# An encoder trunk in which the Strassen token blocks of the FFN become quarters of each half

## The chip, the cores and the metric

The kernel runs on one core of a Trainium2 chip. The metric is the device time of one launch in microseconds (us); the kernel before was timed in three runs. TensorE (PE) multiplies matrices and accumulates in eight PSUM banks; VectorE (DVE), ScalarE (ACT) and GpSimd (POOL) do the elementwise work, POOL without access to PSUM; SyncE (SP) issues the DMAs between HBM and the on-chip memory (SBUF). Each engine takes its instructions in the order of its own queue.

## The reference, cut

1024 tokens, model width 1024, two layers (differential attention, then neighbourhood attention), FFN width 2816, fp32.

```python
h = x
for i in range(DEPTH):
    hn = rmsnorm(h, norm_mix[i])
    ...
    h = h + mix                       # mix = attention output @ w_o
    h = h + swiglu(rmsnorm(h, norm_ffn[i]), ffn_w_gate[i], ffn_w_up[i], ffn_w_down[i])
    gate = jax.nn.sigmoid(rmsnorm(h, norm_ple[i]) @ ple_w_gate[i])
    h = h + gate * (p[i] @ ple_w_proj[i])
return rmsnorm(h, norm_final)
```

`swiglu(h)` is `(silu(h @ w_gate) * (h @ w_up)) @ w_down`.

## The kernel before

Activations lie with features on the 128 partitions and tokens along the free dimension: `h` is eight tiles of [128, 1024], handled in two halves of 512 tokens. An fp32 operand is split into a rounded part and a remainder (`split`: a cast on ACT or POOL, then a subtraction on DVE), and every product of 128x128 weights with 512 tokens is three passes on PE (`PASSES`).

*Output projection.* Attention makes eight head pairs `u`; each pair's output goes to DRAM (`ot`), the last stays in SBUF (`self.last`). `out_proj_first` multiplies the first six pairs (`EARLY`) by their part of `w_o` for both halves, while the last heads are still at work, adds the residual and stores to `hp`. `out_proj` does the last two pairs: first all eight output tiles of half 0, then those of half 1, and behind each half its norm (`norm_blocks`). `norm` sums the squares of the eight tiles on DVE, takes the inverse root and broadcasts it by a PE product (`sums`, `bc`), and makes the normed tiles one by one.

*Gate and up* (`gate_up`) are products by Strassen's scheme in seven products instead of eight (`ORDER`, `seven`): weights are cut into 2x2 blocks (`blocks`), and so are the normed activations, the rows being feature tiles k and k + 4, the columns the two token halves. So five of the seven operands `bt[b]` need half 1. For each of eleven pairs of hidden tiles there are two groups (gate, up) of 84 products of 512 columns; `hand_over` forms the seven operands of down and stores them to DRAM (`ad`), seven DMAs of 512 KB a pair.

*Down* (`down`) works in five chunks of hidden pairs: for each it loads the operands `b` (22 buffers, 14 loads for a chunk of two pairs) and then for four pairs of output tiles the raw weights, which `blocks` turns into seven.

*What sets the order.* Tiles come from pools. Pools take addresses as a stack from the left of SBUF, or with `side="right"` from the right, and give them back when they close; a tile takes slot 0 of its tag first and then the last slot downwards. All DMAs are issued on SP's one queue. A planner orders each engine's queue ahead of time, from costs of its own; among what it holds ready, earlier in the program goes first. In the built program the first instruction of a pool stands, without an exception, behind the last instruction of every earlier pool whose addresses it takes; `reuse_waits="tile"` makes an instruction wait at run time only for the tiles that it overlaps itself. In `gate_up`, `gw` (raw weights and split weights) lies at the bottom of the left stack, over `ob` (`self.last`), `ho` (h of the output projection) and `no` (its norm); `gt` (gates and the other small tiles) lies above, over `oin` (operands and weights of the late products) and `so` (their staging tiles). In `down`, `h` and `pw` lie over `gw`; `db` (operands) over `gt` and three of the `bt` tiles; `dw` (raw and split weights) over `bt` tiles alone.

Lines of the change: `norm` 114, `norm_blocks` 147, `out_proj_first` 554 (its products are L572, its adds L574), `out_proj` 578 (L597), `gate_up` 604 (L631), `down` 690 (L719, loads L706 and L710), `build`. Helpers record one line for many tiles: L101, L103 and L104 are the splits, L190 the blocks of weights.

## Time and profile before

| | us |
|---|---|
| median of three runs | 3028.1 (3024.58 to 3028.22) |
| the profiled execution | 3023.98, its span 3022.2 |
| PE busy | 2739.8 (91%) |
| PE weight loads busy | 2255.1 (75%) |
| DVE busy | 2130.2 (70%) |
| ACT busy | 1217.8 (40%) |
| POOL busy | 1325.6 (44%) |
| DMA | 379.59 MB, 126 GB/s over the span |

A share is an average over stages. PE runs through most of the span without a gap; where it stands still is seen in the timeline, that is the list of an engine's instructions in order of time, neighbours of one kind merged. A line there has the start, the time from the first to the last of the merged ones, engine, line, operation, what is written and read, and in brackets the idle time before and whom the engine waited for. In the window table the figure behind an engine is its busy time in that stretch and in parentheses the instructions.

### The profile page before, as it was taken

How to read it: one execution, taken by the hardware profiler on the slowest of the kernel's cores; microseconds unless marked ns; L12 is line 12 of the kernel's file. 1: busy time of each engine (PE TensorE's matmuls, PEld its weight loads, DVE VectorE, ACT ScalarE, POOL GpSimd, SP SyncE). 2: the span in 40 equal slices, each digit the busy share in tenths (PEclk: the TensorE clock that was granted, in tenths of full speed). 3: DMA queues.
4: the chain of work that ended last, by engine and by line, in shares of the span. 5: the costliest groups of instructions: out<-in, count | busy, mean ns of one | idle time of the engine just before them, and what ended most of it. 6: DMA issues, size and time to landing. Idle time of an engine off the chain costs nothing. (4 is left out here: it accounts for less than half of the span.)

```text
span 3022.2 us, 38402 instructions
## 1 busy us (share of the span) xinstructions
PE 2739.8 (91%) x13272; PEld 2255.1 (75%) x13272; DVE 2130.2 (70%) x3947; ACT 1217.8 (40%) x2534; POOL 1325.6 (44%) x1240
## 2 busy tenths in 40 slices
PE   6999999997599999599997999999399999789998
PEld 5787888885477878478786888888287788567876
DVE  6798878776767666498584666765866667568766
ACT  4454546443444443233332544542344344323241
POOL 1344443431555555477221443432255555457621
PEclk8999999998799999799998999999699999989999
DMA  3001010324244443866132112144333444486312
GB/s 114 28 29 42 29 42 27 147 100 160 63 153 141 145 154 133 313 258 251 35 119 82 54 69 75 47 170 163 117 116 143 153 153 153 159 330 252 138 63 105
DMA packets 106321, 379.59 MB, mean 126 GB/s; under 512 B 12176, under 2 KB 14352, under 8 KB 102032
## 3 DMA queue, kind: packets, MB, share of 16 engines
q1 hardware_dynamic: 106128, 377.15, 34.5%
q8 instruction: 105, 1.72, 0.2%
q14 instruction: 88, 0.72, 0.1%
HBM read 256.52 MB, written 120.59 MB: 125 GB/s over the span
## 5 line engine op out<-in xcount | busy, mean ns | idle before, releaser
L631 PE MATMUL mm<-bt,w 128*128 128x512 f32 x3696 | 870.4, 397 | 62.6 <-ACT w L101 59.6
L631 PEld LDWEIGHTS mm<-bt,w 128*128 128x128 f32 x3696 | 695.2, 189 | 240.2 <-ACT w L101 62.7
L719 PE MATMUL mm<-b,w 128*128 128x512 f32 x1848 | 432.8, 395 | 72.0 <-DMA b<-ad 63.2
L719 PEld LDWEIGHTS mm<-b,w 128*128 128x128 f32 x1848 | 348.1, 190 | 156.8 <-issue 65.2
L104 DVE TENSOR_TENSOR w<-raw,w 128x512 fp32r<-128x512 f32 (+2 forms) x420 | 356.2, 865 | 50.8 <-ACT w L101 50.4
L219 PE MATMUL d<-hnT,w 128*128 128x512 f32 x1536 | 386.3, 399 | 0.0
L219 PEld LDWEIGHTS d<-hnT,w 128*128 128x128 f32 x1536 | 287.0, 189 | 64.3
L101 ACT CAST w<-raw 128x512 fp32r<-128x512 f32 (+2 forms) x420 | 210.6, 527 | 213.0 <-POOL raw L190 109.2
L103 POOL TENSOR_SCALAR w<-st 128x1024 fp32r<-128x1024 f32 (+2 forms) x120 | 134.3, 1121 | 335.5 <-PE mm L219 100.9
L294 PE MATMUL d<-w,hnT 128*128 128x256 f32 x1536 | 227.2, 294 | 16.0 <-POOL w L103 7.7
L294 PEld LDWEIGHTS d<-w,hnT 128*128 128x128 f32 x1536 | 210.5, 198 | 27.7 <-POOL w L103 9.3
L725 POOL TENSOR_TENSOR h<-h,u 128x512 f32<-128x512 f32 x120 | 169.4, 1426 | 119.0 <-DVE u L725 118.4
L104 DVE TENSOR_TENSOR w<-s,w 128x512 fp32r<-128x512 f32 (+2 forms) x168 | 123.4, 749 | 126.4 <-ACT w L101 126.4
L190 POOL TENSOR_TENSOR s<-raw 128x512 f32<-128x512 f32 (+2 forms) x84 | 95.3, 1134 | 267.2 <-DMA raw<-gu 221.0
L366 ACT ACTIVATE e<-e,mx 128x1024 f32<-128x1024 f32 x128 | 147.3, 1151 | 124.7 <-DVE mx L364 113.4
L104 DVE TENSOR_TENSOR w<-st,w 128x1024 fp32r<-128x1024 f32 (+2 forms) x120 | 136.7, 1141 | 82.4 <-POOL w L103 81.4
L219 PE MATMUL mm<-hnT,w 128*128 128x512 f32 x768 | 188.5, 406 | 4.8 <-ACT hnT L101 3.2
L219 PEld LDWEIGHTS mm<-hnT,w 128*128 128x128 f32 x768 | 147.1, 193 | 45.4 <-issue 7.4
L101 ACT CAST at<-tr 128x512 fp32r<-128x512 f32 (+2 forms) x288 | 132.0, 481 | 106.2 <-PE tr L515 67.5
L281 PE MATMUL s<-kh,qs 128*128 128x512 f32 (+2 forms) x384 | 153.4, 409 | 23.2 <-DVE mx L358 12.6
L104 DVE TENSOR_TENSOR at<-tr,at 128x512 fp32r<-128x512 f32 (+2 forms) x288 | 155.7, 550 | 22.5 <-ACT at L101 16.7
L381 POOL TENSOR_SCALAR e<-e,rc 128x1024 f32<-128x1024 f32 x64 | 74.2, 1160 | 217.3 <-DVE rc L379 212.1
(144 smaller groups left out, 4608.1 us busy)
## 6 DMA issues: line engine op xcount, KB each, us to landing
ad<-put SPq DMA_DIRECT2D x154, 512.0 KB, 2.8
b<-ad SPq DMA_DIRECT2D x154, 512.0 KB, 8.4
raw<-gu SPq DMA_DIRECT2D x88, 512.0 KB, 4.8
raw<-wd SPq DMA_DIRECT2D x32, 512.0 KB, 7.3
st<-wpg SPq DMA_DIRECT2D x32, 512.0 KB, 3.6
ot<-ot SPq DMA_DIRECT2D x14, 1024.0 KB, 3.9
o<-ot SPq DMA_DIRECT2D x14, 1024.0 KB, 7.9
st<-da_qk SPq DMA_DIRECT2D x16, 512.0 KB, 3.4
```

Source lines behind the costliest of these rows:

```text
L101: hi_engine.copy(out=w[0], in_=src)
L103: hi_engine.tensor_scalar(out=w[0], in0=src, scalar1=1.0, scalar2=0.0, op0=ALU.mult, op1=ALU.add)
L104: self.nc.vector.tensor_tensor(out=w[1], in0=src, in1=w[0].bitcast(F32), op=ALU.subtract)
L190: nc.gpsimd.tensor_tensor(out=o, in0=x, in1=y, op=op)
L219: self.nc.tensor.matmul(ps, w[:, i, kt * P:(kt + 1) * P], self.hnT[half][:, j, kt, :], start=kt == 0 and n == 0, stop=kt == KT - 1 and n == 2)
L281: self.nc.tensor.matmul(s, qs[:, m, qc], (kh, kl)[part][:, m, kc], start=part == 0, stop=part == 1)
L294: self.nc.tensor.matmul(ps, self.hnT[t // 4][:, i, k, c], ws[k // 4][:, j, (k % 4) * 256:(k % 4 + 1) * 256], start=k == 0 and n == 0, stop ...
L366: nc.scalar.activation(out=e[m], in_=e[m], func=AF.Exp, bias=mx[:, m:m + 1], scale=SLOPES[h], accum_out=sm[:, m:m + 1])
L381: nc.gpsimd.tensor_scalar(out=e[0], in0=e[0], scalar1=rc[:, 0:1], scalar2=0.0, op0=ALU.mult, op1=ALU.add)
L631: nc.tensor.matmul(acc, w[b][:, i, k * P:(k + 1) * P], bt[b][:, j, k], start=first and k == 0 and n == 0, stop=k == 3 and n == 2, skip_gro ...
L719: nc.tensor.matmul(acc, w[b][:, i, q], mv[b, q][:, j], start=first and q == 0 and m == 0, stop=q == n - 1 and m == 2, skip_group_check=True)
L725: eng.tensor_tensor(out=o, in0=x, in1=y, op=ALU.add)
```

## The change

- **Token blocks.** The columns of the 2x2 blocks are no longer the two halves but the first and second quarter (256 tokens) within each half. So each half gives its own part of all seven `bt[b]`, now [128, 2, 4, 2, 256]; a product still takes 512 columns, a quarter from each half. `norm_blocks` is the same for both halves: it works on two tiles at a time, subtracts on DVE, and five of a norm's seven sums of squares go to POOL (`adder`).
- **First pair in parts.** For pair 0 of gate and up the groups run on half 0 first (`part` 0: 256 columns, gate, then up), then on half 1.
- **Output projection.** `out_proj_first` does half 0 alone. `out_proj` then does half 0's last two pairs and half 0's norm, and after that half 1 with all eight pairs, with weights read row-wise (`wn`, a second copy of `w_o`) in two passes over four output tiles each, three weight buffers and two staging buffers; then half 1's norm.
- **Down.** `db` is opened on the right, in the place of `bt`, and chunk 0's loads are issued ahead of `h`, `pT` and `wpp`, which `between` loads. `bt` is allocated in the order in which its tiles are last used.
- **Buffers** of `gate_up`: `raw` 3 to 2, split weights 10 to 14, `p5` and `u3` 2 to 1, `put` 3 to 2. With these sizes `gw` lies over all of `ob`, `ho`, `no` and the first tiles of `oin`; `gt` over the rest of `oin` and `so`. In `down` `h`, `pw` and the staging tile lie over `gw`, `dw` over `gt`, `dt` and `db` over `bt`. `so` (staging of the late weights) lies over attention's values.

```diff
-                nc.vector.tensor_tensor(out=acc[:, :w], in0=acc[:, :w], in1=sq[:, :w], op=ALU.add)
+                eng = adder if adder is not None and k < 6 else nc.vector
+                eng.tensor_tensor(out=acc[:, :w], in0=acc[:, :w], in1=sq[:, :w], op=ALU.add)
...
+        held = {}
+
+        def alloc(k):
+            if k % 2 == 0:
+                held[k // 4] = pool.tile([P, 2, HALF], F32, tag=f"n{k // 4}", name="n", bufs=2)
+            return held[k // 4][:, k % 2]
...
+            ks = slice(k % 4 - 1, k % 4 + 1)
+            lo, up = held[0], held[1]
+            b11, b12, b21, b22 = lo[:, :, :QUART], lo[:, :, QUART:], up[:, :, :QUART], up[:, :, QUART:]
+
+            def put(b, x):
+                self.split((bt[b][:, 0, ks, half], bt[b][:, 1, ks, half]), x, nc.scalar)
+
+            def sub(o, x, y):
+                nc.vector.tensor_tensor(out=o, in0=x, in1=y, op=ALU.subtract)
+
+            put(0, b11)
+            t2 = pool.tile([P, 2, QUART], F32, tag="t2", name="t2", bufs=1)
+            t3 = pool.tile([P, 2, QUART], F32, tag="t3", name="t3", bufs=1)
+            sub(t3, b22, b12)
+            sub(b12, b12, b11)
+            sub(t2, b22, b12)
+            put(5, t2)
+            put(4, b12)
+            put(1, b21)
+            put(6, t3)
+            sub(b21, b21, t2)
+            put(3, b21)
+            put(2, b22)
+
+        self.norm(h, c, i, pool, sink, order=(0, 1, 4, 5, 2, 3, 6, 7), alloc=alloc, adder=nc.gpsimd)
```

```diff
+            o = p.tile([P, 2, HALF], F32R, tag=f"o{u}", name="o")
+            nc.sync.dma_start(out=o.bitcast(F32), in_=self.ot[layer][u, :, :, :HALF])
...
+            r = p.tile([P, HALF], F32, tag="r", name="r", bufs=3)
+            nc.sync.dma_start(out=r, in_=self.residual(layer, dt)[:, :HALF])
+            acc = psd.tile([P, HALF], F32, tag="d", name="d")
...
+        last = self.last.rearrange("p l b q -> p l (b q)")
+        late = range(EARLY, PAIRS)
+        os = {}
+        for half, u in [(0, u) for u in late[:-1]] + [(1, u) for u in range(PAIRS - 1)]:
+            o = op.tile([P, 2, HALF], F32R, tag=f"o{half}{u}", name="o")
+            nc.sync.dma_start(out=o.bitcast(F32), in_=self.ot[layer][u, :, :, half * HALF:(half + 1) * HALF])
+            os[half, u] = o
+        for half in range(2):
+            os[half, PAIRS - 1] = last[:, :, half * HALF:(half + 1) * HALF]
+        h = {}
...
+                h[dt, half] = hpool.tile([P, HALF], F32, tag="h", name="h", bufs=12)
+                nc.sync.dma_start(out=h[dt, half], in_=self.hp[dt] if half == 0 else self.residual(layer, dt)[:, c])
...
+            if half == 0:
+                for dt in range(KT):
+                    w = self.weights(wo[dt, :, EARLY * P:], op, "w", cols=len(late) * P, bufs=3)
+                    acc = ps.tile([P, HALF], F32, tag="mm", name="mm")
+                    for u in late:
+                        k = u - EARLY
+                        product(acc, w[:, :, k * P:(k + 1) * P], u, k == 0, u == PAIRS - 1)
+                    done(dt, acc)
+            else:
+                for q in range(2):
+                    accs = [ps.tile([P, HALF], F32, tag="mm", name="mm") for _ in range(4)]
+                    for u in range(PAIRS):
+                        w = self.weights(wn[u * P:(u + 1) * P, q * HALF:(q + 1) * HALF], op, "w", cols=HALF, bufs=3)
+                        for d in range(4):
+                            product(accs[d], w[:, :, d * P:(d + 1) * P], u, u == 0, u == PAIRS - 1)
+                    for d in range(4):
+                        done(4 * q + d, accs[d])
+            self.norm_blocks(lambda k, c, half=half: h[k, half], half, 3 * layer + 1, np, bt)
```

```diff
-                    r = wp.tile([P, 2, HALF], F32, tag="raw", name="raw", bufs=3)
+                    r = wp.tile([P, 2, HALF], F32, tag="raw", name="raw", bufs=2)
...
-            def group(pr, which):
-                w = prepare(pr, which)
+                    gates[pr] = tp.tile([P, 2, 2, 2, QUART], F32, tag="gt", name="gt", bufs=2)
+                return self.blocks(raw[0][:, 0], raw[0][:, 1], raw[1][:, 0], raw[1][:, 1], wp, "w", [HALF], 14)
+
+            def block(gt, f, t, part):
+                return gt[:, f, :, t] if part is None else gt[:, f, part, t]
...
+                t = {k: tp.tile([P, 2, QUART], F32, tag=k, name=k, bufs=n)
+                     for k, n in (("p1", 2), ("p5", 1), ("u2", 2), ("u3", 1))}
+                cut = (lambda x: x) if part is None else (lambda x: x[:, part])
+                t = {k: cut(x) for k, x in t.items()}
...
-                            nc.tensor.matmul(acc, w[b][:, i, k * P:(k + 1) * P], bt[b][:, j, k],
+                            nc.tensor.matmul(cut(acc), w[b][:, i, k * P:(k + 1) * P], cut(bt[b][:, j, k]),
...
-                    o = tp.tile([P, 2, HALF], F32R, tag="put", name="put", bufs=3)
+                    o = tp.tile([P, 2, 2, QUART], F32R, tag="put", name="put", bufs=2)
...
+                if pr == 0:
+                    ws = [prepare(pr, which) for which in range(2)]
+                    for part in range(2):
+                        for which in range(2):
+                            group(pr, which, ws[which], part)
+                else:
+                    for which in range(2):
+                        group(pr, which, prepare(pr, which))
```

```diff
+                if chunk is CHUNKS[0]:
+                    between()
...
-                bt = [bp.tile([P, 2, 4, HALF], F32R, tag=f"b{b}", name=f"bt{b}") for b in range(7)]
+                bt = {b: bp.tile([P, 2, 4, 2, QUART], F32R, tag=f"b{b}", name=f"bt{b}") for b in ORDER}
...
+                    self.out_proj(layer, wo, wn, hp, ps, np, op, bt)
...
+                bp = tc.alloc_tile_pool(name=f"db{layer}", bufs=1, side="right", reuse_waits="tile")
+                pt, wpp = [], []
...
+
+                    def between():
+                        for dt in (0, 4, 1, 5, 2, 6, 3, 7):
+                            nc.sync.dma_start(out=h[dt], in_=self.hd[dt])
+                        for k in range(2):
+                            pt.append(self.weights(a["pT"][layer, k], pw, f"pt{k}"))
+                            wpp.append(self.weights(a["wpp"][layer, k], pw, f"wp{k}"))
+
+                    self.down(layer, h, ps, bp, between)
+                bp.release()
```

## Rows read from the trace of the kernel before

**Rows 1.** Groups by line: busy us, mean ns | idle us before, its releasers.

```profile
L631 PE MATMUL mm<-bt,w 128*128 128x512 f32 x3696 | 870.4, 397 | 62.6 <-ACT w L101 59.6 <-ACT p L644 1.5 <-DVE w L104 1.1
L719 PE MATMUL mm<-b,w 128*128 128x512 f32 x1848 | 432.8, 395 | 72.0 <-DMA b<-ad 63.2 <-DVE u L725 3.8 <-ACT w L101 3.8
```

**Rows 2.** PE timeline, layer 0: start us, us, what [idle before <-releaser].

```profile
701.24 3.12 PE L395 MATMUL av<-at,v 128*128 128x256 f32 x24
...
705.46 4.64 PE L597 MATMUL mm<-o,w 128*128 128x512 f32 x18
711.12 4.39 PE L597 MATMUL mm<-ot,w 128*128 128x512 f32 x18 [1.02 <-ACT ot L101]
...
730.82 0.95 PE L126 MATMUL sums<-mean,acc 128*128 128x1 f32 x8
...
749.57 1.83 PE L126 MATMUL sums<-mean,acc 128*128 128x1 f32 x8 [14.37 <-DVE acc L123]
753.75 2.04 PE L134 MATMUL bc<-diag,ones 128*128 128x512 f32 x2 [2.34 <-DVE diag L132]
785.58 1.22 PE L631 MATMUL mm<-bt,w 128*128 128x512 f32 x2 [29.79 <-ACT w L101]
```

**Rows 3.** Timeline of DVE, layer 0, the two norms.

```profile
735.87 5.35 DVE L137 SCALAR_TENSOR_TENSOR n<-h,g,bc 128x512 f32<-128x512 f32 x8
...
741.73 4.29 DVE L104 TENSOR_TENSOR bt<-n,bt 128x512 fp32r<-128x512 f32 x7
...
759.81 5.10 DVE L104 TENSOR_TENSOR bt<-n,bt 128x512 fp32r<-128x512 f32 x3
```

**Rows 4.** Timeline of ACT (ScalarE), the last split of the norm.

```profile
784.39 0.62 ACT L101 CAST bt<-n 128x512 fp32r<-128x512 f32 x1 [1.10 <-POOL n L174]
784.91 0.61 ACT L101 CAST w<-raw 128x512 fp32r<-128x512 f32 x1
```

**Rows 5.** Timeline of SP, the first weights of gate and up.

```profile
732.15 64.50 SPq L616 DMA_DIRECT2D raw<-gu  x5
```

**Rows 6.** Timeline of PE, layer 1, early products and entry to gate and up.

```profile
2096.99 15.09 PE L572 MATMUL d<-o,w 128*128 128x512 f32 x64
...
2188.49 1.22 PE L631 MATMUL mm<-bt,w 128*128 128x512 f32 x2 [29.79 <-ACT w L101]
```

**Rows 7.** Windows, L572 alone: stretch, length, PE busy (count), clock, DMA, GB/s.

```profile
560.00:643.00 83.00, 37.71 (x142) 1.00 0.42 158
...
2015.00:2072.00 57.00, 36.89 (x141) 1.00 0.67 256
```

**Rows 8.** Windows: length, PE, PEld, DVE, ACT, POOL busy (count), clock, DMA.

```profile
260.00:340.00 80.00, 70.95 (x438) 58.30 (x438) 73.55 (x190) 47.91 (x98) 31.55 (x36) 1.00 0.08 28
643.00:705.00 62.00, 61.36 (x338) 52.37 (x336) 46.33 (x107) 25.61 (x52) 23.39 (x31) 1.00 0.30 106
2072.00:2097.00 25.00, 25.00 (x128) 20.98 (x128) 14.78 (x39) 5.54 (x16) 6.86 (x13) 1.00 0.49 167
```

**Rows 9.** Timeline of PE, layer 0, entry to down.

```profile
1199.67 22.33 PE L631 MATMUL mm<-bt,w 128*128 128x512 f32 x95
1251.53 4.71 PE L719 MATMUL mm<-b,w 128*128 128x512 f32 x12 [29.53 <-DMA b<-ad]
1256.65 0.94 PE L719 MATMUL mm<-b,w 128*128 128x512 f32 x3 [0.41 <-DMA b<-ad]
...
1264.24 15.94 PE L719 MATMUL mm<-b,w 128*128 128x512 f32 x69 [0.32 <-DMA b<-ad]
```

**Rows 10.** Timeline of SP, the same.

```profile
1222.17 0.32 SPq L671 DMA_DIRECT2D ad<-put  x1
...
1228.20 0.33 SPq L710 DMA_DIRECT2D raw<-wd  x1
...
1245.90 9.67 SPq L706 DMA_DIRECT2D b<-ad  x12
```

**Rows 11.** Timeline of POOL, the first use of down's weights.

```profile
1238.60 0.72 POOL L190 TENSOR_TENSOR s<-raw 128x256 f32<-128x256 f32 x1 [8.57 <-DMA raw<-wd]
```

More of the change, by code (lines that the diff above doesn't have):

```diff
@@ L111, in weights, with norm @@
         return w
-    def norm(self, h, c, i, pool, sink, order=range(KT), keep=None):
+    def norm(self, h, c, i, pool, sink, order=range(KT), alloc=None, adder=None):
         nc = self.nc
@@ L135, in norm @@
         for k in order:
-            n = keep[:, k] if keep is not None else pool.tile([P, HALF], F32, tag="n", name="n", bufs=4)
+            n = alloc(k) if alloc else pool.tile([P, HALF], F32, tag="n", name="n", bufs=4)
             nc.vector.scalar_tensor_tensor(out=n[:, :w], in0=h(k, c), scalar=self.g[:, i, k:k + 1],
@@ L149, in norm_blocks @@
         c = slice(half * HALF, (half + 1) * HALF)
-        def put(b, k, x):
-            self.split((bt[b][:, 0, k], bt[b][:, 1, k]), x, nc.scalar)
-        if half == 0:
-            self.n0 = pool.tile([P, KT, HALF], F32, tag="n0", name="n0", bufs=1)
-            self.norm(h, c, i, pool, lambda k, n: put(k // 4, k % 4, n), keep=self.n0)
-            return
-        n0, held = self.n0, {}
+        held = {}
[3 more added lines that the diff above has]
+            return held[k // 4][:, k % 2]
@@ L160, in sink @@
         def sink(k, n):
-            if k < 4:
-                held[k] = n
+            if k % 4 not in (1, 3) or k < 4:
                 return
-            k -= 4
-            n11, n21, n12, n22 = n0[:, k], n0[:, k + 4], held.pop(k), n
-            put(2, k, n22)
-            nc.gpsimd.tensor_tensor(out=n11, in0=n12, in1=n11, op=ALU.subtract)
-            put(4, k, n11)
-            nc.gpsimd.tensor_tensor(out=n12, in0=n22, in1=n12, op=ALU.subtract)
-            put(6, k, n12)
-            t2 = pool.tile([P, HALF], F32, tag="t2", name="t2", bufs=2)
@@ L564, in out_proj_first @@
             w = self.weights(wo[dt, :, :EARLY * P], self.slab, "slab", cols=EARLY * P)
-            r = p.tile([P, S], F32, tag="r", name="r", bufs=3)
-            nc.sync.dma_start(out=r, in_=self.a["xp"][dt] if layer == 0 else self.hs[dt])
-            for half in range(2):
-                c = slice(half * HALF, (half + 1) * HALF)
-                acc = psd.tile([P, HALF], F32, tag="d", name="d")
-                for k in range(EARLY):
-                    for n, (i, j) in enumerate(PASSES):
-                        nc.tensor.matmul(acc, w[:, i, k * P:(k + 1) * P], os[k][:, j, c], start=k == 0 and n == 0,
-                                         stop=k == EARLY - 1 and n == 2)
-                nc.vector.tensor_tensor(out=r[:, c], in0=acc, in1=r[:, c], op=ALU.add)
+            r = p.tile([P, HALF], F32, tag="r", name="r", bufs=3)
@@ L575, in out_proj_first @@
+            nc.sync.dma_start(out=r, in_=self.residual(layer, dt)[:, :HALF])
+            acc = psd.tile([P, HALF], F32, tag="d", name="d")
+            for k in range(EARLY):
+                for n, (i, j) in enumerate(PASSES):
+                    nc.tensor.matmul(acc, w[:, i, k * P:(k + 1) * P], os[k][:, j], start=k == 0 and n == 0,
+                                     stop=k == EARLY - 1 and n == 2)
+            nc.vector.tensor_tensor(out=r, in0=acc, in1=r, op=ALU.add)
             nc.sync.dma_start(out=self.hp[dt], in_=r)
@@ L576, in out_proj_first, with residual, out_proj @@
         p.release()
-    def out_proj(self, layer, wo, h, ps, np, op, bt):
+    def residual(self, layer, dt):
+        return self.a["xp"][dt] if layer == 0 else self.hs[dt]
+    def out_proj(self, layer, wo, wn, hpool, ps, np, op, bt):
         nc, tc = self.nc, self.tc
-        late = PAIRS - EARLY
-        os = []
-        for k in range(late - 1):
-            o = op.tile([P, 2, S], F32R, tag=f"o{k}", name="o")
-            nc.sync.dma_start(out=o.bitcast(F32), in_=self.ot[layer][EARLY + k])
-            os.append(o)
-        os.append(self.last.rearrange("p l b q -> p l (b q)"))
-        ws = []
-        for dt in range(KT):
-            ws.append(self.weights(wo[dt, :, EARLY * P:], op, f"w{dt}", cols=late * P))
-            nc.sync.dma_start(out=h[dt], in_=self.hp[dt])
+        last = self.last.rearrange("p l b q -> p l (b q)")
[8 more added lines that the diff above has]
+        h = {}
@@ L811, in build @@
                     self.stage = sb.enter_context(tc.tile_pool(name=f"so{layer}", bufs=2, reuse_waits="tile"))
-                    h = [hp.tile([P, S], F32, tag=f"h{t}", name=f"h{t}") for t in range(KT)]
-                    self.out_proj(layer, a["da_wo"] if layer == 0 else a["na_wo"], h, ps, np, op, bt)
+                    wo, wn = (a[("da_wo", "na_wo")[layer]], a[("da_wn", "na_wn")[layer]])
+                    self.out_proj(layer, wo, wn, hp, ps, np, op, bt)
             self.gate_up(layer, ps, bt)
```

89 lines of the change are left out of this document (37 added, 52 removed).

## The prediction

> **What bounds the kernel now.** The table of engines says TensorE (PE): busy 91% of the span. The groups by line say where the rest is: the products of gate and up (L631) sat idle 62.6 us, 59.6 of it until a weight split on ScalarE, and those of down (L719) 72.0, 63.2 of it until an operand load [rows 1]. Both come twice, once a layer. So I read PE in order of time around the two places.
>
> *Entry to gate and up.* Attention's last value products end at 704.4, the late output products run from 705.5 to 730.8, and the first product of gate and up starts at 785.6; between are only the small products of two norms, the second held 14.4 us for a sum on VectorE (DVE) [rows 2]. DVE shows why: after half 0's norm factor it makes eight normed tiles and splits them, 0.61 to 0.67 us an operation, and half 1's sums stand behind [rows 3]. From half 1's norm factor (755.8) to the first product are 29.8 us, DVE splitting and subtracting. ScalarE's order is the telling one: the first weight cast of gate and up (784.91) stands right behind the last cast of `bt` (784.39) [rows 4], though its load was issued at 732.15 [rows 5]. The planner queued the new stage behind the whole old stage, not behind the one tile whose place it takes. Layer 1 has the same entry (first product at 2188.5), and 64 early products in one run at the end of its attention, to 2112.1, as nothing else was left [rows 6].
>
> *Entry to down.* PE ends at 1222.0, starts at 1251.5 and crawls until 1264.2: 30 products in 12.7 us [rows 9]. The raw weights were used from 1238.6 [rows 11]; the operands were issued from 1245.9, after the last store of the hand-over [rows 10].
>
> **The change part by part.** A product of 512 columns costs (15.09 − 0.39)/63 = 0.2333 us [rows 1, 6].
>
> *Early output products, half 1 taken out:* 144 of 288 a layer, 33.6 us of PE. They are filler beside the last heads, so the gain is what attention can shrink. In before half of them (142 and 141; a few records can be missing) are done by 643 in layer 0 and 2072 in layer 1 [rows 7]. From there, layer 0 has 62 us and 46.33 of DVE, less eight adds at 0.67 is 41; the busiest DVE beside attention was 73.55 of 80, 0.92 [rows 8]: 44.4 us, a gain of 17.6 (12 to 22). Layer 1 has 25 us to attention's end with 14.78 of DVE, less four adds is 12: 13 us by DVE, 15 with the chain of the last blocks; gain 10 (8 to 13). Its run of 64 afterwards goes too.
>
> *Half 0's late products:* now 48. `last` was ready 5.7 us after attention, the products ahead of it hidden in that [rows 2]. With three weight buffers nine can go ahead; the other 39 take 9.1. With some wait for weights I take 15.5 us (13 to 18). Their staging tiles now lie over attention's values, so the loads queue behind the last value product.
>
> *Half 1 whole:* 192 products, 44.8 us, plus 2.5 for half 0's sums and broadcast. Their 16 weights need a split on POOL and one on DVE each. DVE has half 0's norm then: 8 normed tiles, 8 subtractions (moved here from POOL), 14 splits, 30 operations at 0.65 = 19.5 us, starting 5.0 after the sums [rows 2, 3] = about 7.5 after half 0's products. They come earlier in the program than the weights, and in before DVE let half 0's norm pass ahead of half 1's sums (the 14.4 us). By then about four weights can be split (three buffers and one refilled, the first ready 1.6 after half 0): 11.2 us of products, to +12.8; the norm holds DVE to +27; 14 us of PE wait. DVE's gaps will let some split in: I take 12 (0 to 16). POOL's five norm sums per half are hidden beside half 0's products; for half 1 they are in the tail.
>
> *Tail:* half 1's norm, nothing beside it. 3.4 us for the last adds, squares and sums, 5.0 to the broadcast, 30 operations at 0.65, one for the cast: 29 us (27 to 39, the upper end by the 31 us that 32 of them took beside POOL's subtractions). Pair 0 in quarters was meant to cover this: part 0 needs half 0 alone. But `gw` (two raw and fourteen weight buffers, from the bottom of the left stack) lies over `ho`, `no` and `oin`, which live until half 1's norm ends; by the order of rows 4 the first weight cast stands behind that norm again.
>
> *Quarter products:* 336 of 256 columns for 168 of 512. 24 of 256 took 3.12 us [rows 2]: 0.118 to 0.130 each; at 0.123, 41.3 against 39.2, +2.1 (0.5 to 4.5). The Trainium skill, "TensorE: Matmul & The Clock Gate", section "Back-to-back issue gap", gives sustained 81 ns for 128 columns and 131 for 512; between them 256 would cost three quarters of 512, an estimate from that page, and the quarters 19.6 us a layer more. The trace does not agree: here 256 costs 0.53 of 512.
>
> Sum from attention's end to gate and up: 15.5 + 44.8 + 2.5 + 12 + 29 = 103.8. Before: 785.6 − 705.5 = 80.1 and 2188.5 − 2097.0 = 91.5 [rows 2, 6]. Layer 0: 103.8 − 17.6 − 80.1 + 2.1 = +8.2. Layer 1: 103.8 − 10 − 91.5 + 2.1 = +4.4.
>
> *Down.* `db` now lies over `bt` alone and is issued from PE's last product; `h` and `pw` lie over `gw`, also free then. But the raw weights (`dw`) now lie over `gt`, in use until the hand-over's last store, and come later in the program than `between()`'s loads. On SP's one queue they stand behind 13 operands (one can go early), 6 stores, 8 tiles of `h` and one of `pT`: they are the 29th of 512 KB. Operands arrived every (1264.24 − 1256.65)/6 = 1.27 us [rows 9]; in before the raw load was the tenth since 1222.17 [rows 10] and used 16.4 us after it [rows 11], 3.7 above 10 × 1.27. After: 29 × 1.27 + 3.7 + 1.5 for the split = 42 us from PE's end, against 29.5. The crawl goes (12.7 − 7.0, less 1.9 for the slow first twelve products = 3.8) as the operands are all there. Net +9 a layer (−3, if the raw loads pass `h`, to +20, if chunk 1's eight operands pass them too).
>
> *Hidden:* fewer buffers in gate and up (`raw` 2, `put` 2, `p5` and `u3` 1). A group takes 84 × 0.2333 = 19.6 us, and 14 weight buffers hold two whole groups, so PE has a group in hand; 0 (to +5 in all, if `put` blocks ScalarE).
>
> Total: 8.2 + 4.4 + 18 = +30.6 on the profiled execution's 3024.0 us, which lies 4.1 below the median of the runs (3028.1): 3058.7, so 3059.
>
> **The rivals.** *The splits keep up* (about no change): if the planner interleaves half 1's weight splits with half 0's norm, DVE's 35 us (30 operations, 16 splits and eight adds at 0.65) fit into 47, and the 24 us of starving are gone: 3035; with attention's gains at their upper ends 3027. For: there is room. Against: in before the later norm's sums waited. It decides from the point where the norm holds DVE longer than the products in hand last, 11.2 us.
>
> *Tile by tile* (faster): the new stage enters as each tile comes free. Gate and up would start when its raw weights are in, some 9 us into the tail instead of 29, part 0 covering the rest, and down's raw weights would pass the loads of `h`, 27 instead of 42. 2 × (20 + 15): 2989. For: operands are issued with no store between them. Against: rows 4, and slots that hold `no`'s tiles to the end.
>
> *Down's queue is longer:* chunk 1's eight operands also pass the raw weights, 2 × 8 × 1.27 = 20 more: 3079. For: they need only `bt` free.
>
> **How the numbers follow.** Forecast 50%, splits keep up 20%, tile by tile 10%, longer queue 20%. A measurement of this kernel can tell about 0.2% (6 us) from no change. Faster (under 3022): all of tile by tile, a fifth of splits keep up (if the tail or down comes out at its lower bound too) and 4% of the forecast: 16%. Within: a third of splits keep up and 6% of the forecast: 10%. Slower 74%. The forecast alone reaches from 3035 to 3085; the range to leave 2 in 10 out: 3016 to 3090.
>
> **What would show it.** PE's timeline: attention's end 18 and 10 us earlier; in half 1's products a stall of about 12 us until a split on DVE; from the last of them to the first of gate and up 29 us, ended by ScalarE's first weight cast right behind the last of `bt`; 0.12 us a quarter product; down's first product some 42 us after gate and up's last, ended by the raw weights, not by an operand. A first gate product that runs while half 1's norm is still on DVE makes the forecast wrong, as does an SP queue with raw weights ahead of `h`.

## The result, and the profile after

The changed kernel takes 3102.9 us (median of four runs, 3101.9 to 3107.4) against 3026.3 for the kernel before: a ratio of 1.0257, 95% interval 1.024 to 1.0275, some 77 us slower. The prediction was 3059 with a range to 3090: slower, as forecast, and by two and a half times as much.

| | after |
|---|---|
| the profiled execution | 3101.98, its span 3100.2 |
| PE busy | 2777.7 (90%) |
| PE weight loads busy | 2286.3 (74%) |
| DVE busy | 2136.6 (69%) |
| ACT busy | 1220.8 (39%) |
| POOL busy | 1373.9 (44%) |
| DMA | 379.66 MB, 122 GB/s over the span |

The span is 78 us longer: PE is busy for 38 us more and idle for 40 us more (POOL has 48 us more to do, but is idle more than half of the time). So the loss is gaps of PE and, for about as much, products that cost more; only 336 of PE's records are new, those of the quarters. One reason for dearer products is PE's granted clock, which switches between 1.2 and 2.4 GHz and stood at 0.948 of full speed in the mean, after 0.956 before. Groups by line (busy us, mean ns | idle before, its releasers), to be read against [rows 1]; L669 is gate and up, L765 down, L615 the late output products:

```profile
L669 PE MATMUL mm<-bt,w 128*128 128x512 f32 (+1 forms) x4032 | 877.2, 379 | 47.0 <-ACT w L102 41.4 <-DVE u L686 5.1
L765 PE MATMUL mm<-b,w 128*128 128x512 f32 x1848 | 439.8, 399 | 109.9 <-ACT w L102 105.2 <-DVE h L771 3.2 <-DVE u L771 0.8
L615 PE MATMUL mm<-o,w 128*128 128x512 f32 x384 | 104.1, 420 | 22.1 <-POOL w L104 13.0 <-DVE w L105 8.9 <-DVE sq L416 0.2
```

Down's idle time went from 72.0 to 109.9 us and has another releaser: a weight cast on ScalarE, not an operand's load. Gate and up's fell from 62.6 to 47.0, and the late products, which stood still for under 3 us before, now wait 22.1.

PE's timeline of layer 0, from attention's end to gate and up, against [rows 2]:

```profile
690.31 0.70 PE L412 MATMUL msp<-sq,ones 128*128 128x256 f32 x2 [0.85 <-ACT sq L410]
...
709.69 0.86 PE L615 MATMUL mm<-ot,w 128*128 128x512 f32 x3
711.58 3.02 PE L615 MATMUL mm<-o,w 128*128 128x512 f32 x12 [1.03 <-POOL w L104]
...
752.12 10.97 PE L615 MATMUL mm<-o,w 128*128 128x512 f32 x40 [3.12 <-DVE w L105]
762.92 2.88 PE L615 MATMUL mm<-ot,w 128*128 128x512 f32 x12
770.94 1.84 PE L128 MATMUL sums<-mean,acc 128*128 128x1 f32 x8 [5.14 <-DVE acc L125]
778.16 2.04 PE L136 MATMUL bc<-diag,ones 128*128 128x512 f32 x2 [5.38 <-DVE diag L134]
...
798.86 3.31 PE L669 MATMUL mm<-bt,w 128*128 128x256 f32 x12 [18.66 <-ACT w L102]
...
816.50 15.66 PE L669 MATMUL mm<-bt,w 128*128 128x256 f32 x123 [1.24 <-ACT w L102]
```

Attention ends 14.8 us earlier, half 0's late products last to 710.55, half 1's to 765.80, and then PE stands still for 33 us but for the norm's small products. ACT's timeline has the same picture as [rows 4], the first cast of gate and up right behind the last of `bt`:

```profile
797.67 0.62 ACT L102 CAST bt<-n 128x512 fp32r<-128x512 f32 x1 [0.58 <-DVE n L171]
798.19 0.61 ACT L102 CAST w<-raw 128x512 fp32r<-128x512 f32 x1
```

PE at the entry to down in both layers, against [rows 9]:

```profile
1189.68 55.23 PE L669 MATMUL mm<-bt,w 128*128 128x512 f32 x236
1297.49 1.22 PE L765 MATMUL mm<-b,w 128*128 128x512 f32 x2 [52.58 <-ACT w L102]
...
2732.40 1.22 PE L765 MATMUL mm<-b,w 128*128 128x512 f32 x2 [52.59 <-ACT w L102]
```

And SP's queue in that gap, from the first long run of operands on, against [rows 10]:

```profile
1247.26 5.12 SPq L750 DMA_DIRECT2D b<-ad  x7
1253.37 0.32 SPq L711 DMA_DIRECT2D ad<-put  x1
1255.00 4.17 SPq L750 DMA_DIRECT2D b<-ad  x4
1260.17 4.08 SPq L874 DMA_DIRECT2D h<-hd  x4
1265.22 0.32 SPq L711 DMA_DIRECT2D ad<-put  x1
1266.46 4.15 SPq L874 DMA_DIRECT2D h<-hd  x4
1271.58 0.33 SPq L109 DMA_DIRECT2D st<-pT  x1
1272.86 9.22 SPq L750 DMA_DIRECT2D b<-ad  x8
1283.10 1.60 SPq L711 DMA_DIRECT2D ad<-put  x2
1285.65 0.33 SPq L109 DMA_DIRECT2D st<-wpp  x1
1286.89 1.61 SPq L756 DMA_DIRECT2D raw<-wd  x2
```

Ahead of the raw weights go the operands of chunk 0 (eleven of the fourteen in this stretch), eight tiles of h, pT, *eight operands of chunk 1*, the last stores and wpp. The stage table puts it together; every figure is a difference of starts in PE's timeline (the last product of gate and up by its end):

| us | layer 0 before | after | | layer 1 before | after | |
|---|---|---|---|---|---|---|
| to attention's last product | 705.1 | 690.3 | -14.8 | 623.5 | 611.6 | -11.9 |
| from there to gate and up's first | 80.5 | 108.6 | +28.1 | 91.5 | 109.0 | +17.5 |
| gate and up | 436.4 | 446.1 | +9.6 | 437.1 | 440.9 | +3.8 |
| gap to down's first product | 29.5 | 52.6 | +23.1 | 29.7 | 52.6 | +22.9 |
| down | 222.0 | 220.8 | -1.1 | 223.3 | 223.4 | +0.1 |

(Layer 1 is counted from the first product behind layer 0's down.) With 0.7 us at the end this is the whole difference of the spans, 78.0 us.

### The profile page after: what moved, and what is told of

Its sections match the earlier page's. It is cut to its first block, busy times and chain, and to the rows that moved or that the text cites. A ratio compares the mean times of both kernels' runs of the same rounds, so it can differ in the third digit from the quotient of the medians.

```text
span 3100.2 us, 39266 instructions
## 1 busy us (share of the span) xinstructions
PE 2777.7 (90%) x13608; PEld 2286.3 (74%) x13608; DVE 2136.6 (69%) x3989; ACT 1220.8 (39%) x2550; POOL 1373.9 (44%) x1274
## 2 busy tenths in 40 slices
DMA packets 118838, 379.66 MB, mean 122 GB/s; under 512 B 13168, under 2 KB 15344, under 8 KB 116336
## 5 line engine op out<-in xcount | busy, mean ns | idle before, releaser
L669 PE MATMUL mm<-bt,w 128*128 128x512 f32 (+1 forms) x4032 | 877.2, 379 | 47.0 <-ACT w L102 41.4
L669 PEld LDWEIGHTS mm<-bt,w 128*128 128x128 f32 x4032 | 718.5, 190 | 208.0 <-ACT w L102 46.0
L765 PE MATMUL mm<-b,w 128*128 128x512 f32 x1848 | 439.8, 399 | 109.9 <-ACT w L102 105.2
L765 PEld LDWEIGHTS mm<-b,w 128*128 128x128 f32 x1848 | 350.5, 190 | 199.3 <-ACT w L102 106.0
L105 DVE TENSOR_TENSOR w<-raw,w 128x512 fp32r<-128x512 f32 (+2 forms) x420 | 369.0, 892 | 82.1 <-ACT w L102 81.0
L104 POOL TENSOR_SCALAR w<-st 128x1024 fp32r<-128x1024 f32 (+3 forms) x152 | 171.8, 1132 | 455.3 <-PE d L229 67.3
L105 DVE TENSOR_TENSOR w<-st,w 128x1024 fp32r<-128x1024 f32 (+3 forms) x152 | 167.6, 1104 | 131.3 <-POOL w L104 131.1
L291 PE MATMUL s<-kh,qs 128*128 128x512 f32 (+2 forms) x384 | 156.4, 415 | 24.2 <-DVE mx L368 12.5
L200 POOL TENSOR_TENSOR raw<-raw,s 128x512 f32<-128x512 f32 (+2 forms) x84 | 103.0, 1226 | 147.2 <-DVE w L105 147.2
```

The lines of the kernel that those rows point to most:

```text
L104: hi_engine.tensor_scalar(out=w[0], in0=src, scalar1=1.0, scalar2=0.0, op0=ALU.mult, op1=ALU.add)
L105: self.nc.vector.tensor_tensor(out=w[1], in0=src, in1=w[0].bitcast(F32), op=ALU.subtract)
L200: nc.gpsimd.tensor_tensor(out=o, in0=x, in1=y, op=op)
L291: self.nc.tensor.matmul(s, qs[:, m, qc], (kh, kl)[part][:, m, kc], start=part == 0, stop=part == 1)
L669: nc.tensor.matmul(cut(acc), w[b][:, i, k * P:(k + 1) * P], cut(bt[b][:, j, k]), start=first and k == 0 and n == 0, stop=k == 3 and n == 2 ...
L765: nc.tensor.matmul(acc, w[b][:, i, q], mv[b, q][:, j], start=first and q == 0 and m == 0, stop=q == n - 1 and m == 2, skip_group_check=True)
```

## The experiments

The theory after the result: four separate losses. Down's raw weights wait in SP's queue; one raw buffer fewer starves the start of gate and up; two staging tiles starve the late output products; and the pools of gate and up lie over the norm's, so the parts of pair 0 cover nothing. Against each stands a rival of its own.

### Down as before, everything else changed

```diff
-                if chunk is CHUNKS[0]:
-                    between()
...
+            bp = st.enter_context(tc.tile_pool(name=f"db{layer}", bufs=1, reuse_waits="tile"))
...
+                for dt in (0, 4, 1, 5, 2, 6, 3, 7):
+                    nc.sync.dma_start(out=h[dt], in_=self.hd[dt])
```

> The changed kernel (3102.9 us) with down as in the kernel before: operand pool on the left, h, pT and wpp issued ahead of it, and everything else of the change kept. Theory (the raw weights of down wait behind thirty loads and the last stores on SP's queue): the gap of PE at the entry to down falls from 52.6 us to about 30 in each layer, the crawl of 3 us returns: 3102.9 - 2 x 20 = 3063 (3057 to 3069). Rival (the two store buffers `put` hold the hand-over up, wherever the operands lie): ScalarE goes on waiting about 10 us three times for its stores and the gap stays over 42: 3083 or more.

Measured: 3057.9 us (3056.4 to 3059.1), ratio to before 1.0115 (1.010 to 1.013). PE's timeline:

```profile
1278.61 1.62 PE L764 MATMUL mm<-b,w 128*128 128x512 f32 x3 [32.14 <-DMA b<-ad]
```

The gap is 32.1 us and ended by an operand again, with two store buffers still in place. So the edit of down alone costs 45.0 of the 76.6 us, and the store buffers are not what does it. Some 41 us of it are the two gaps (32.1 and 31.8 us here instead of 52.6); down itself also got shorter, to 218.8 and 219.2 us from 220.8 and 223.4, for a reason that the section on the prediction gives.

### Down alone, in the kernel before

```diff
-            bp = st.enter_context(tc.tile_pool(name=f"db{layer}", bufs=1, reuse_waits="tile"))
...
+                bp = tc.alloc_tile_pool(name=f"db{layer}", bufs=1, side="right", reuse_waits="tile")
...
+                    self.down(layer, h, ps, bp, between)
```

> The kernel before (3026.3 us) with the change of down alone: operands on the right in the place of `bt`, chunk 0's loads ahead of h, pT and wpp; three store buffers as before. Theory (the queue): the gap at the entry to down grows from 29.5 to about 52 us, the crawl goes: 3026.3 + 2 x 21 = 3068 (3058 to 3074). Rival (two store buffers are what holds the raw weights back): with three of them the last store goes out early and the gap stays under 42: 3026 to 3045.

Measured: 3070.2 us (3067.8 to 3072.5), ratio 1.0155 (1.014 to 1.0171): +45.1. PE and SP:

```profile
1274.98 1.22 PE L720 MATMUL mm<-b,w 128*128 128x512 f32 x2 [51.00 <-ACT w L101]
```

```profile
1251.61 9.19 SPq L705 DMA_DIRECT2D b<-ad  x8
1261.82 0.32 SPq L671 DMA_DIRECT2D ad<-put  x1
1263.10 0.33 SPq L108 DMA_DIRECT2D st<-pT  x1
1264.33 1.66 SPq L711 DMA_DIRECT2D raw<-wd  x2
```

The same gap with three store buffers, and the same eight operands of chunk 1 ahead of the raw weights. From both sides the step is worth 45 us.

### Down over memory that really comes free early, in the kernel before

One pool for each of the seven `bt` tiles, in the order of last use; the split weights of gate and of up in a pool of seven each (`ga`, `gb`), raw weights in `gr`. Down's operands lie over the `bt` pools, seven tiles of h over `gb`, raw and eight split weights over `gr` and `ga`; only pT, wpp, one tile of h and the staging tile lie over the gates. The first raw weights are issued ahead of the operands. To make room, `raw` has two buffers, `put` two, `p5` and `u3` one, as in the changed kernel.

```diff
+            wb, tp, wp, wa = open_pool("gb"), open_pool("gt"), open_pool("gr"), open_pool("ga")
...
+                new = lambda: (wa, wb)[which].tile([P, 2, HALF], F32R, tag="w", name="w", bufs=7)
...
+                bps = [tc.alloc_tile_pool(name=f"bt{layer}_{b}", bufs=1, side="right", reuse_waits="tile")
+                       for b in ORDER]
...
+            load(CHUNKS[0], 0)
+            load(CHUNKS[0], 1)
```

> The kernel before (3026.3 us) with one pool for each operand tile of gate and up, the split weights of gate and of up in two pools of seven, raw weights in a pool of their own, and down's operands, raw and split weights and h laid over those of them that come free first; h and the first raw weights lie nowhere over the pool of the gates. Raw weights of down's first two groups are issued ahead of the operands. Theory (the planner holds back a pool's first instruction behind the whole of each older pool whose addresses it takes, so what counts is what a pool lies over): raw weights and most operands of chunk 0 are issued before PE's last product of gate and up, and the gap falls from 29.5 us to under 10 in each layer: about 3026.3 - 2 x 24 = 2978 (2966 to 2996). Rival (the 14 operands and the hand-over's seven stores fill the queue whatever their order, 21 x 1.27 us): the gap stays over 20: 3010 or more.

Measured: 3002.0 us (3001.1 to 3004.3), ratio 0.9931 (0.9914 to 0.9947). SP and PE:

```profile
1210.10 1.21 SPq L703 DMA_DIRECT2D raw<-wd  x2
1219.48 7.68 SPq L718 DMA_DIRECT2D b<-ad  x12
```

```profile
1179.62 56.63 PE L633 MATMUL mm<-bt,w 128*128 128x512 f32 x242
1236.09 15.56 PE L737 MATMUL mm<-b,w 128*128 128x512 f32 x66
```

The second line has no bracket: PE goes from gate and up into down without a pause, and down's idle time over both layers is 15.8 us instead of 72.0. The rival (the queue is full whatever its order) falls. But the gain was 23 us and not 48, outside what was expected, because other stretches got longer: gate and up began 33.31 us after the norm's broadcast instead of 29.79, and took 444.8 us instead of 436.4, with about the same in layer 1; and down itself took 228.0 and 228.7 us instead of 222.0 and 223.3.

```profile
791.31 50.11 PE L633 MATMUL mm<-bt,w 128*128 128x512 f32 x204 [33.31 <-ACT w L101]
...
853.87 361.38 PE L633 MATMUL mm<-bt,w 128*128 128x512 f32 x1541 [4.85 <-DVE u L648]
```

### Pair 0 whole

```diff
-                if pr == 0:
-                    ws = [prepare(pr, which) for which in range(2)]
-                    for part in range(2):
-                        for which in range(2):
-                            group(pr, which, ws[which], part)
-                else:
-                    for which in range(2):
-                        group(pr, which, prepare(pr, which))
+                for which in range(2):
+                    group(pr, which, prepare(pr, which))
```

> The changed kernel (3102.9 us) with pair 0 of gate and up in whole products of 512 columns, not in parts. Theory (the parts cover nothing, since no weight of gate and up is ready before half 1's norm ends; they cost 2.4 us of quarter products a layer and the waits that follow): first gate product at the same distance from the last output product (33 us), gate and up 9 and 3 us shorter: 3091 (3088 to 3098). Rival (part 0 does hide part of half 1's norm): slower than 3103, up to 3120.

Measured: 3103.7 us (3103.1 to 3111.0), no difference from the changed kernel; my 3091 was wrong, and so was the rival. Gate and up still took 444.6 and 440.7 us (446.1 and 440.9 with parts). The quarters cost about a microsecond and cover nothing; the other 8 and 4 us of that stage come from something else, and layer 0's excess has the same face as in the run before, a wait for an eviction in the third group:

```profile
865.69 383.34 PE L669 MATMUL mm<-bt,w 128*128 128x512 f32 x1631 [6.33 <-DVE u L686]
```

POOL's timeline of the same run, some 15 us earlier, suggests a reason, which the next run tests. POOL waits for raw weights, and the addition that an eviction needs (L693) stands behind that wait in its queue:

```profile
847.67 1.29 POOL L200 TENSOR_TENSOR s<-raw 128x512 f32<-128x512 f32 x1 [6.36 <-DMA raw<-gu]
848.92 1.29 POOL L693 TENSOR_TENSOR p<-p,u 128x512 f32<-128x512 f32 x1
```

### Three raw buffers

```diff
-                    r = wp.tile([P, 2, HALF], F32, tag="raw", name="raw", bufs=2)
+                    r = wp.tile([P, 2, HALF], F32, tag="raw", name="raw", bufs=3)
...
-                return self.blocks(raw[0][:, 0], raw[0][:, 1], raw[1][:, 0], raw[1][:, 1], wp, "w", [HALF], 14)
+                return self.blocks(raw[0][:, 0], raw[0][:, 1], raw[1][:, 0], raw[1][:, 1], wp, "w", [HALF], 13)
```

> The changed kernel with pair 0 whole (as in e5_whole_pair, 3103.7 us) and with three raw buffers and thirteen split ones instead of two and fourteen. Theory (two raw buffers make the loads of gate and up's second and third groups late, GpSimd waits for them and holds the eviction and PE): the stage of gate and up falls from 444.6 and 440.7 us to about 437 in both layers as before the change, so 3103.7 - 11 = 3093 (3088 to 3097). Rival (the single `p5` and `u3` or the late start of the weights are what holds PE): the stage stays over 443 in layer 0 and the time over 3099.

Measured: 3087.4 us (3084.8 to 3093.6), ratio 1.0205 (1.019 to 1.022): 16.4 under the run with pair 0 whole. Gate and up took 435.6 and 436.2 us, as before the change, with `p5` and `u3` still single. That is 9.0 + 4.5; another 3 us a layer came out of the tail, where the broadcast now waited 2.35 us instead of 5.38 (see the last section). Together that is 19.5, more than the 16.4; other stages differ by a few us from build to build (attention's end in layer 0, for one, by up to 5).

### Own pools and three raw buffers, in the kernel before

```diff
-                    r = wp.tile([P, 2, HALF], F32, tag="raw", name="raw", bufs=2)
+                    r = wp.tile([P, 2, HALF], F32, tag="raw", name="raw", bufs=3)
...
-                new = lambda: (wa, wb)[which].tile([P, 2, HALF], F32R, tag="w", name="w", bufs=7)
+                def new():
+                    m = count[0] % 13
+                    count[0] += 1
+                    return (wb if 4 <= m < 11 else wa).tile([P, 2, HALF], F32R, tag="w", name="w",
+                                                            bufs=7 if 4 <= m < 11 else 6)
```

> As e4_own_pools (3002.0 us), with three raw buffers and thirteen split weights in pools of seven and six. In e4_own_pools PE no longer stood still at the entry to down, but gate and up took 444.8 us instead of 436.4 and began 3.5 us later after the norm. Theory (that was the second raw buffer's doing): gate and up back to about 437 in both layers, no gap at down: 3002.0 - 2 x 8 - up to 7 = 2982 (2978 to 2990). Rival (the split of the weights into two pools is what slowed gate and up): 2998 or more.

Measured: 2983.0 us (2981.9 to 2984.0), ratio 0.9857 (0.9842 to 0.9872). Gate and up are back at 437.2 and 437.3 us and down still begins without a gap, so having two pools of weights is not what cost the time (how the tiles are dealt out to the two was changed along with the buffer). The start of gate and up stays 3.9 us late a layer (33.69 for 29.79): its raw weights were issued at 785.76, not at 732.15 as in [rows 5], which fits a place over the norm's last tiles.

### Pools that leave the norm alone, in the changed kernel

Down as in the two runs before; raw weights, gate's split weights and `p1`, `p5`, `u2`, `u3` lie over the operands and the staging of the output projection only.

```diff
+            wb, tp, gp, wp, wa = (open_pool(k) for k in ("gb", "gt", "gp", "gr", "ga"))
...
+                t = {k: gp.tile([P, 2, QUART], F32, tag=k, name=k, bufs=1) for k in ("p1", "p5", "u2", "u3")}
```

> The changed kernel (3102.9 us) with down's pools as in e4_own_pools, and with the raw weights, the split weights of gate and the four small tiles of a group in pools that lie over the operands and staging of the output projection alone, not over h and the norm. Theory (the parts of pair 0 covered nothing because the pool of the weights lay over the norm's): gate's part 0, 84 products of 256 columns, runs while half 1's norm is still on VectorE, its first product under 15 us after the last output product instead of 33; half 1's norm gets some 5 us longer by the splits of those weights; the stage from attention's end to the end of gate and up shrinks by 5 to 8 us a layer; down's gap goes: 3102.9 - 2 x 50 - 2 x 6 = 2991 (2980 to 3003). Rival (the weights can't be ready earlier for other reasons, such as VectorE's queue or the loads): first product still 30 us or more after the last output product, 3003 to 3010.

Measured: 3000.3 us (2999.6 to 3009.6), ratio 0.9924 (0.9907 to 0.9941). PE's timeline:

```profile
769.33 3.23 PE L670 MATMUL mm<-bt,w 128*128 128x256 f32 x12 [3.35 <-ACT w L102]
772.36 1.06 PE L128 MATMUL sums<-mean,acc 128*128 128x1 f32 x8
775.26 5.82 PE L670 MATMUL mm<-bt,w 128*128 128x256 f32 x30 [1.84 <-ACT w L102]
780.92 1.02 PE L136 MATMUL bc<-diag,ones 128*128 128x512 f32 x2
```

The last output product ends at 765.98; the first gate product follows after 3.4 us, not 33, and gate's part 0 runs around half 1's sums and broadcast. From attention's end to gate and up's end it is 543.1 us instead of 554.6 in layer 0, 543.8 instead of 549.9 in layer 1. So the parts of pair 0 can run beside the norm, and what voided that was which pool lay over which. It does not make the new order a gain yet: before the change that stretch was 516.9 and 528.6 us, and attention ends only some 15 and 11 us earlier. From 769.3 to 835.0 PE was busy for 50.8 of 65.7 us, at a granted clock of 0.82.

### Four staging tiles

```diff
-                h[dt, half] = hpool.tile([P, HALF], F32, tag="h", name="h", bufs=12)
+                h[dt, half] = hpool.tile([P, HALF], F32, tag="h", name="h", bufs=10)
...
-                    self.stage = sb.enter_context(tc.tile_pool(name=f"so{layer}", bufs=2, reuse_waits="tile"))
+                    self.stage = sb.enter_context(tc.tile_pool(name=f"so{layer}", bufs=4, reuse_waits="tile"))
```

> The changed kernel (3102.9 us) with four staging tiles for the weights of the late output products instead of two, and ten buffers for h of the output projection instead of twelve. Theory (two staging tiles make the weights' loads late, and these starve the late products of half 0 and half 1): their waits, 22.1 us over both layers, fall to under 10: 3091 (3086 to 3096). Rival (VectorE and the three weight buffers hold them): 3100 to 3106.

Measured: 3087.1 us (3085.7 to 3087.6), ratio 1.0200 (1.0185 to 1.0215): 15.8 less than the changed kernel. The group of the late products:

```profile
L615 PE MATMUL mm<-o,w 128*128 128x512 f32 x384 | 97.8, 406 | 10.8 <-DVE w L105 7.1 <-POOL w L104 3.5 <-DVE sq L416 0.2
```

Its waits for POOL's casts fall from 13.0 to 3.5 us, those for DVE hardly (8.9 to 7.1), so to 10.8 in all, just over the ten that were expected; its busy time falls too, from 104.1 to 97.8; from attention's end to the last output product layer 0 needs 66.7 us instead of 75.5.

### The norms' sums on DVE

```diff
-        self.norm(h, c, i, pool, sink, order=(0, 1, 4, 5, 2, 3, 6, 7), alloc=alloc, adder=nc.gpsimd)
+        self.norm(h, c, i, pool, sink, order=(0, 1, 4, 5, 2, 3, 6, 7), alloc=alloc)
```

> The changed kernel (3102.9 us) with the sums of squares of the output projection's norms on VectorE, as before the change, instead of five of seven on GpSimd. Theory (in half 1's norm, where nothing lies beside it, a sum on GpSimd takes 1.3 us against 0.6 on VectorE, and the chain of adds and sums after the last product, 5.1 us, goes back to 3.4): 3102.9 - 3 = 3100 (3096 to 3103). Rival (the ten sums a layer that go back to VectorE delay its splits for half 1's products): 3105 to 3115.

Measured: 3094.7 us (3091.3 to 3096.8), ratio 1.0221 (1.0205 to 1.0236): 8.2 less, outside both expectations. The chain that the theory spoke of did not get shorter: the sums still waited 4.96 us (5.14). What fell were the waits of the late products, to 14.2 us:

```profile
L615 PE MATMUL mm<-o,w 128*128 128x512 f32 x384 | 99.7, 406 | 14.2 <-POOL w L104 10.8 <-DVE w L105 3.2
```

The waits for DVE's part of the splits went (8.9 to 3.2), although DVE has more to do. A likely reading is that POOL's sums and DVE's subtractions hold each other up (last section); it was not tested by itself.

### All at once

The changed kernel with the pools that leave the norm alone, four staging tiles, ten h buffers and three raw buffers.

```diff
+            wb, tp, gp, wp, wa = (open_pool(k) for k in ("gb", "gt", "gp", "gr", "ga"))
...
+                    r = wp.tile([P, 2, HALF], F32, tag="raw", name="raw", bufs=3)
...
+                    self.stage = sb.enter_context(tc.tile_pool(name=f"so{layer}", bufs=4, reuse_waits="tile"))
```

> The changed kernel with what the runs before it pointed to at once: down's pools and the pools of gate and up as in e8_tail_pools (3000.3 us), four staging tiles and ten buffers for h as in e9_staging4 (15.8 us under the changed kernel), three raw buffers as in e6_raw3 (16.4 us under e5_whole_pair). If the three losses lie in different stretches, they add up: 3000.3 - 16 - 10 = 2974 (2968 to 2982), below e7_own_pools_raw3 (2983.0). Rival (the parts of pair 0, now begun in the tail, already hide what the second raw buffer cost): 2984.

Measured: 2975.4 us (2970.6 to 2977.0), ratio 0.9829 (0.9813 to 0.9846). The losses are separate and nearly add up, and this version beats both kernels. PE at the entry to down:

```profile
1179.70 45.42 PE L669 MATMUL mm<-bt,w 128*128 128x512 f32 x194
1224.97 15.57 PE L781 MATMUL mm<-b,w 128*128 128x512 f32 x66
```

Gate and up end 3.0 us later than before the change in layer 0 (1225.0 against 1222.0) and, counted from the end of layer 0's down, 5.5 earlier in layer 1. So the new token blocks with their order of the output projection are about even; nearly the whole gain of 51 us is the gap at down, 59 us over both layers, of which down itself gives back 10 (228.5 and 226.7 us instead of 222.0 and 223.3). The kernel before with its own pools and three raw buffers stood at 2983.0 us: of the change as such, 8 us are left.

## Why the prediction was right in its sign and wrong in its size

The sum failed first at down, where the queue ahead of the raw weights was counted too short (28 of the 47 us that the span missed by), then at the buffers, put at nothing, and at half 0's late products. Term by term:

*Attention's gain: right.* Forecast 17.6 and 10, measured 14.8 and 11.9, both within their ranges. In layer 0 the other seven builds with this attention end it between 689.9 and 694.7, so a gain of 10 to 15 us; the forecast was at the upper end.

*Half 0's late products: too low.* 15.5 forecast, 20.2 (690.31 to 710.55) and 21.5 measured. "Some wait for weights" was there, but sized as if three weight buffers were the limit; the two staging tiles behind them are worth 3 to 4 us of it, as with four of them it took 17.2 and 17.3. Another part is the price of a product, taken as 0.2333 us: the 39 products behind `last` came to 12.5 us of PE and not 9.1, at a granted clock of 0.83 (696.6 to 710.6), behind a stretch in which PE kept pausing for 0.5 to 1.9 us. Before the change these products ran without long waits, at 1.00 (705.4 to 731.0).

*Half 1: too high, and the mechanism with it.* 59.3 forecast, 55.2 and 54.4 measured. The 12 us of starving were 6.6 and 4.8. The step that failed here, to the prediction's luck, as it offset 9 us of the other misses, is "in before DVE let half 0's norm pass ahead": DVE's queue of the changed kernel has a weight split every few operations of the norm, so DVE never held PE for more than 3.1 us. This half of "the splits keep up" was right; its time of 3035 was not, since the other losses came.

*Tail: mechanism right, 4 us short.* 29 forecast, 33.1 in both layers, ended by the weight cast behind the last of `bt` as said. The excess is the chain of adds and sums (5.1 instead of 3.4) and the four `diag` operations.

*Quarter products: right.* 123 of them took 15.66 us, 0.127 each, and the run with pair 0 whole puts their price at 1.5 and 0.2 us a layer (446.1 against 444.6, 440.9 against 440.7). By the prediction's estimate from the Trainium skill, "TensorE: Matmul & The Clock Gate", section "Back-to-back issue gap", they would have been 19.6 us a layer dearer; the trace does not agree.

*Fewer buffers, "0 (to +5 in all)": wrong.* It reasoned from the steady state, where 14 split buffers hold two groups. At the start there is nothing in hand: with two raw buffers the second group's loads wait for the first's splits. Gate and up grew by 9.6 and 3.8 us; with pair 0 whole 8.2 and 3.6 of it were left, and the third raw buffer took 9.0 and 4.5 off.

*Down: the largest miss, 28 us.* The gap was forecast at 42 us and measured at 52.6. The step that failed is the count of SP's queue: 28 loads and stores ahead of the raw weights, where the trace has 37 since 1245.04, chunk 1's eight operands and a `wpp` among them. The rival "down's queue is longer" names the cause, eight more operands at 1.27 us: 42 + 10.2 = 52.2. That down's edit costs this is shown from both sides; that it is these eight is argued from the count, as no run takes just them out. I had weighed the rival at 20%, with no reason against it; the order among loads follows what is free, and `bt` was. The same rule that I had used for `db` against `dw` decides here, and I did not apply it to chunk 1.

The credit of 3.8 us for the crawl failed as well (1.1 and -0.1), although the crawl went: PE's waits within down fell from 6.7 to 1.9 us in layer 0 and from 6.1 to 2.8 in layer 1. What ate it is the price of a product, which the prediction took as unchanged. Down's products in the run with down as before, then in that with down alone:

```profile
L764 PE MATMUL mm<-b,w 128*128 128x512 f32 x1848 | 431.5, 394 | 70.8 <-DMA b<-ad 68.8 <-DVE w L105 1.8
L720 PE MATMUL mm<-b,w 128*128 128x512 f32 x1848 | 441.1, 400 | 109.5 <-ACT w L101 102.2 <-DVE h L726 5.9 <-DVE w L104 0.8
```

From 1400 to 1490, where PE never pauses and the granted clock is 1.00, the first run does 399 products and the second 387, as many as the changed kernel. In the first the operands lie on the left of SBUF, in the other two on the right. At 0.006 to 0.007 us each, 924 products are some 6 us a layer; in the run with down over memory that comes free early, where the operands lie on the right as well, down is 6.0 and 5.4 us longer than before.

Together: down 28, gate and up 9, half 0 11, the tail 8, less 9 for half 1, and small change of 1: 48 us, against a miss of 47 in the span.

The rival's time of 2989 for "tile by tile" counts the crawl's 3.8 us a layer twice (27 against 42 should be 31 against 42), so it should read about 2996; no conclusion hangs on it. "Tile by tile" fell in the traces: nothing of gate and up ran during half 1's norm until the pools were moved apart.

## What to carry to other kernels

When an edit moves a pool, list for every load of the next stage which older pool it lies over and when that pool's last instruction ends, and then write down the whole queue in that order, the next chunk's prefetches too: a prefetch that is free early will pass the load that everyone waits for. Give memory that is freed at different times pools of its own; that alone took the gap at down from 29.5 us to nothing, although down itself then took 5 to 6 us longer. A buffer count that is harmless in the steady state is to be counted again for the first two groups, when nothing is in hand.

## What the runs showed of the hardware

DVE and POOL hold each other up, in both directions. In the tail of layer 0 of the changed kernel the four `diag` operations of DVE ran beside POOL's subtractions; with three raw buffers POOL happened to be idle there, and its first subtraction came later, beside DVE's unbroken run of the norm. DVE and POOL after (timeline), then the same two engines in the run with three raw buffers:

```profile
774.11 3.90 DVE L134 TENSOR_SCALAR diag<-ident,rs 128x128 f32<-128x128 f32 x4 [1.13 <-POOL rs L131]
```

```profile
774.05 1.26 POOL L200 TENSOR_TENSOR s<-raw 128x512 f32<-128x512 f32 x1
775.39 1.32 POOL L200 TENSOR_TENSOR s<-s,raw 128x512 f32<-128x512 f32 x1
```

```profile
774.91 0.87 DVE L134 TENSOR_SCALAR diag<-ident,rs 128x128 f32<-128x128 f32 x4 [1.13 <-POOL rs L131]
```

```profile
785.85 11.29 POOL L200 TENSOR_TENSOR s<-raw 128x512 f32<-128x512 f32 x1 [10.97 <-DMA raw<-gu]
```

Four operations take 3.90 us beside POOL and 0.87 without it, and one subtraction of POOL lasts 11.29 us instead of 1.26 while DVE works without a break. It made the tail 3 us longer a layer than the prediction's 5.0 us from sums to broadcast, and an early start of POOL's weight work was no gain there. The Trainium skill, "SBUF — State Buffer", section "Who interferes with whom", says that DVE and POOL share a pair of ports, which in DVE's 2-port mode whoever issues first holds for the whole instruction while "the other **fully blocks**". The trace agrees that each holds the other up; it shows POOL kept out not for one but for a run of some 17 DVE instructions (785.85 to 797.14).

A product of 512 columns costs 0.233 us with its operands on the right of SBUF and 0.227 with them on the left, at a granted clock of 1.00. The kernel before has both: 395 products of gate and up, operands on the right, took 92.0 us (803.1 to 895.5), and 210 of down, on the left, 47.7 (1425.8 to 1473.5). Down's products went from the lower price to the higher in every run that moved its operands to the right. What about the place makes the difference is open.
